# A two-layer decoder trunk on one core: sums of squares and the mean's spread moved to the matrix engine, convolution taps dealt out anew, the last output projection in halves, three row tiles at each feed-forward's end

## The chip, the cores and the metric

The kernel runs on one core of a Trainium2 chip. A core has a matrix engine (TensorE, PE in the rows), a vector engine (VectorE, DVE), a scalar engine (ScalarE, ACT) and a general engine (GpSimd, POOL), each with its own instruction stream; SyncE (SP) issues the transfers. Engines wait for each other by semaphores only. The metric is the time of one execution on the device, in microseconds (us); a kernel's time is the median of its runs.

## The reference

The input is 512 tokens of 1024 features in float32. Two mixers follow each other, a convolution module and an attention, each followed by a gated feed-forward; every one of the four blocks adds its result to its input, and normalises its input first.

```python
def rmsnorm(x, g):
    y = xf * lax.rsqrt(jnp.mean(xf * xf, axis=-1, keepdims=True) + EPS)
def conformer_conv(h, ...):
    u = h @ w_pw1 + b_pw1
    a, gate = jnp.split(u, 2, axis=-1)
    u = a * jax.nn.sigmoid(gate)
    u = causal_dwconv(u, w_dw, b_dw)          # 31 taps a channel
    u = jax.nn.silu(layernorm(u, ln_g, ln_b)) # mean and variance over features
    return u @ w_pw2 + b_pw2
```

The attention has 16 query heads in 4 groups of four, three branches merged by gates, and an output projection `w_out`. The feed-forward (2816 wide) has a gate, a causal convolution of width 3 and a down-projection back to 1024 features.

## The kernel before, in words

Features lie on the 128 partitions and the 512 tokens along the free axis, so an activation is eight tiles of 128x512, and `x[0..7]` is the residual stream. Every float32 product is made of three matmuls (`mm3`, L240 to L243): both operands are split into a rounded high part (a cast on ACT, L230, L236, L405, L616) and the remainder (a subtraction on DVE or POOL, L231, L237, L406, L617). PSUM tiles come from small rings named `pf`, `pb`, `pa` and `po`.

The Tile framework's scheduler sets the order on each engine: it plays the program through with costs of its own and puts on each engine what is ready first, so an edit at one place moves instructions at others.

- **Norms.** `Norm.add` scales and splits a row tile and squares it on ACT (L265). The first norm (`two=True`) sums the squares in two accumulators, three adds on POOL and three on DVE (L272). `sums` adds over features with one-column matmuls against `ones` (L285), four for each 128x512 tile. Then DVE and POOL make 1/sqrt (L293, L295), and `spread` (L306) transposes it into a row for all partitions.
- **Convolution module.** Eight units of 128 channels. `project_half` makes the first pointwise layer, `U.gate` and `U.unit` the gated input (L358, L364, L365). The 31 taps of a unit are dealt out by the table `CONV`: `pe` gives the groups of four taps that the matrix engine makes with diagonal weights (`products`), `pool` the taps of POOL (L388, from copies scaled by ACT at L386), and what is left goes to DVE (L354). `a`, `b`, `c` say how many DVE taps are written between other steps. `merge` (L436) joins the parts.
- **The convolution's layer norm.** One-column matmuls (L527) sum the last units' values and squares; three matmuls against `avg` (L529) make the mean, spread over the partitions, in `dp`. DVE, POOL and `spread(rs)` make 1/sqrt; `warm(w1)` and `warm(w2)` (L213, L211) put matmuls without use before and behind it. `centre` (L550) and `scale` (L554, L555) lead to the second pointwise layer.
- **Feed-forwards.** `down` makes a row tile of the down-projection in a `pb` bank; at each block's end two row tiles run together: first all products but the last column block, then, for both, the last one, which waits for the block's last activation (L236 from L631).
- **Attention.** A table deals out heads and projections over steps. `out_proj(n)` makes the output projection of one or two groups, row tile by row tile in a `pf` bank; `out2` is that of the last group, ready when both of its half-groups (`os`) are done. `out1` is that of group 2.

## Time and profile before

| | us |
|---|---|
| median of three runs | 1280.56 |
| lowest and highest run | 1279.15, 1282.36 |
| the profiled execution | 1281.02 |
| its span in the trace | 1279.1 |
| PE busy in the span | 1237.5 |
| DVE, ACT, POOL busy | 1008.7, 729.0, 370.4 |

Stages on PE: convolution module to about 190 us, first feed-forward to 553, attention to about 911 (its start overlaps the feed-forward's end), second feed-forward to the end. The profiled execution lies 0.46 us above the median, and 1.9 us of it are outside the span. Timeline rows give start, length, engine, line, operation, output<-inputs, shape, count, and in brackets the engine's idle time before it with what ended that. A float32 matmul with one column or a float32 transpose leaves two records each, so x8 at L285 or L527 is four instructions.

### The profile page before, as it was taken

Reading aid. Unit: us, or ns where it says so; the run is one execution under the profiler, and the core shown is the slowest. Engines: PE = TensorE matmul, PEld = TensorE weight load, DVE = VectorE, ACT = ScalarE, POOL = GpSimd, SP = SyncE. Lnnn points to the kernel's source line nnn. Section 1 sums busy time; section 2 is a strip of 40 time slices with the busy share of each in tenths; the row PEclk is TensorE's granted clock in tenths of the full one; section 3 lists DMA queues with packets and bytes.
Section 4 is the critical chain, followed back from the end, with each engine's and each line's share of the span. In section 5 each row is a group of like instructions: output and inputs, shape, how many; then the busy total and the mean of one; then the engine's idle time right before and its main releaser. Section 6 shows DMA issues by size and latency. Waiting matters only on the chain. (4 is left out here: it accounts for less than half of the span.)

```text
span 1279.1 us, 20179 instructions
## 1 busy us (share of the span) xinstructions
PE 1237.5 (97%) x7447; PEld 1089.2 (85%) x7447; DVE 1008.7 (79%) x1728; ACT 729.0 (57%) x1337; POOL 370.4 (29%) x434
## 2 busy tenths in 40 slices
PE   8999899999999999999889999999899999999998
PEld 6788778879999999978888987877687999999996
DVE  6699957689977787765868888889768997778873
ACT  5766545345654455453767888767544565455541
POOL 1639603001100010051657677634300110001100
PEclk8999989999999999999999999999899999999999
DMA  7555413223232333235431111111122333233321
GB/s 276 165 144 141 107 50 128 73 70 126 88 112 100 99 100 107 77 116 166 134 101 51 34 45 39 34 34 34 51 68 70 110 103 108 90 106 106 97 79 72
DMA packets 43794, 121.91 MB, mean 95 GB/s; under 512 B 5424, under 2 KB 8240, under 8 KB 43696
## 3 DMA queue, kind: packets, MB, share of 16 engines
q1 hardware_dynamic: 43696, 120.64, 30.0%
q8 instruction: 58, 0.95, 0.3%
q14 instruction: 40, 0.33, 0.1%
HBM read 108.04 MB, written 2.10 MB: 86 GB/s over the span
## 5 line engine op out<-in xcount | busy, mean ns | idle before, releaser
L700 POOL TENSOR_TENSOR S<-raw 128x512 f32<-128x512 f32 x34 | 52.8, 1553 | 516.3 <-DMA raw<-in_up_dram 266.0
L616 ACT CAST wh<-raw 128x1024 fp32r<-128x1024 f32 (+2 forms) x112 | 96.0, 863 | 90.3 <-PE pb L242 26.8
L617 DVE TENSOR_TENSOR wl<-raw,wh 128x1024 fp32r<-128x1024 f32 (+2 forms) x112 | 114.8, 1031 | 29.3 <-ACT wh L616 29.1
L241 PE MATMUL pf<-s,wh 128*128 128x512 f32 x296 | 116.8, 405 | 9.7 <-ACT s L236 4.6
L242 PE MATMUL pf<-s,wh 128*128 128x512 f32 x296 | 119.1, 403 | 0.0
L243 PE MATMUL pf<-s,wl 128*128 128x512 f32 x296 | 118.5, 400 | 0.0
L1149 POOL TENSOR_SCALAR s<-s,cf,gates 128x128 f32<-128x128 f32 (+3 forms) x128 | 81.0, 640 | 73.7 <-DVE cf L1146 59.1
L241 PE MATMUL pb<-s,wh 128*128 128x512 f32 x254 | 99.8, 396 | 2.5 <-ACT s L236 2.3
L242 PE MATMUL pb<-s,wh 128*128 128x512 f32 x254 | 100.2, 395 | 0.0
L243 PE MATMUL pb<-s,wl 128*128 128x512 f32 x254 | 99.8, 393 | 0.0
L230 ACT CAST wh<-raw 128x1024 fp32r<-128x1024 f32 (+2 forms) x62 | 63.5, 1024 | 41.5 <-PE pf L242 14.9
L241 PE MATMUL pf<-wh,s 128*128 128x256 f32 (+1 forms) x288 | 83.4, 290 | 3.6 <-DVE v L974 2.0
L1143 ACT ACTIVATE s<-pa,mn 128x128 f32<-128x128 f32 (+3 forms) x128 | 67.4, 531 | 30.4 <-DVE mn L1138 23.2
L242 PE MATMUL pf<-wl,s 128*128 128x256 f32 (+1 forms) x288 | 82.9, 288 | 1.8 <-POOL wl L231 1.4
L231 DVE TENSOR_TENSOR wl<-raw,wh 128x1024 fp32r<-128x1024 f32 (+2 forms) x46 | 60.9, 1325 | 28.6 <-ACT wh L230 28.6
L243 PE MATMUL pf<-wh,s 128*128 128x256 f32 (+1 forms) x288 | 82.4, 286 | 0.0
L241 PEld LDWEIGHTS pf<-s,wh 128*128 128x128 f32 x296 | 56.9, 193 | 23.8 <-ACT s L236 5.3
L236 ACT CAST s<-s 128x512 fp32r<-128x512 f32 x76 | 47.2, 621 | 50.8 <-DVE s L631 38.7
L750 DVE TENSOR_TENSOR x<-pb,x 128x512 f32<-128x512 f32 x80 | 54.0, 686 | 25.1 <-PE pb L243 25.0
L617 DVE TENSOR_TENSOR l<-raw,h 128x1024 fp32r<-128x1024 f32 (+2 forms) x56 | 57.3, 1024 | 17.5 <-ACT h L616 17.4
L1138 DVE CUSTOM_DVE_ANT_0 pa<-pa,tab 128x128 f32<-128x128 f32 (+3 forms) x128 | 62.5, 494 | 11.0 <-PE pa L1133 10.1
L237 DVE TENSOR_TENSOR s<-s,s 128x512 fp32r<-128x512 f32 x76 | 59.2, 779 | 13.9 <-ACT s L236 13.6
(299 smaller groups left out, 3957.7 us busy)
## 6 DMA issues: line engine op xcount, KB each, us to landing
raw<-in_up_dram SPq DMA_DIRECT2D x88, 512.0 KB, 3.6
raw<-in_dn_dram SPq DMA_DIRECT2D x48, 256.0 KB, 2.6
raw<-in_dn_dram SPq DMA_DIRECT2D x32, 320.0 KB, 2.8
raw<-in_pw_dram SPq DMA_DIRECT2D x16, 512.0 KB, 4.7
raw<-in_win_k_dram SPq DMA_DIRECT2D x8, 536.0 KB, 3.5
s<-s SPq DMA_DIRECT2D x32, 128.0 KB, 2.3
raw<-in_win_q_dram SPq DMA_DIRECT2D x8, 512.0 KB, 4.0
raw<-in_cw_dram SPq DMA_DIRECT2D x8, 512.0 KB, 3.4
```

What stands on the lines that cost most here:

```text
L230: nc.scalar.copy(h[:, :n], raw[:, :n])
L231: (eng or nc.vector).tensor_sub(l[:, :n], raw[:, :n], h[:, :n].bitcast(F32))
L237: nc.vector.tensor_sub(l, src, h.bitcast(F32))
L241: nc.tensor.matmul(out, ah, bh, start=start, stop=False)
L242: nc.tensor.matmul(out, ah, bl, start=False, stop=False)
L243: nc.tensor.matmul(out, al, bh, start=False, stop=stop)
L616: nc.scalar.copy(h, raw)
L617: (eng or nc.vector).tensor_sub(l, raw, h.bitcast(F32))
L750: nc.vector.tensor_add(x[m], o[m], x[m])
L1138: nc.vector.tensor_tensor_reduce(sv, sv, mask[:, S - n:S], 1.0, 3e38, op0=ALU.add, op1=ALU.min, accum_out=s.mn[:, c:c + 1])
L1143: nc.scalar.activation(a, sv, AF.Exp, scale=-1.0, bias=s.mn[:, c:c + 1], accum_out=s.sums[:, c:c + 1])
L1149: nc.gpsimd.tensor_scalar(a, a, s.cf[:, c:c + 1], gates[:, i, 3 * s.h + 1 + br:3 * s.h + 2 + br], op0=ALU.mult, op1=ALU.mult)
```

## The change

Five parts, with small changes of tables beside them. (1) In the first norm each squared tile is summed by four one-column matmuls at once; the six adds are gone. (2) `dp` is no longer a product with `avg`: the mean out of `mom` is transposed and spread like 1/sqrt, and the two fillers grow from 10 and 6 to 14 and 10. (3) `CONV` is dealt out anew: PE takes a seventh group of unit 6, POOL 38 taps where it had 47, DVE five more; the low parts of the diagonals of units 6 and 7 and of the first three weight blocks of the second pointwise layer (`"pw2": 3`) go from DVE to POOL. (4) `out_last` makes the last output projection four row tiles at a time, first with the first half-group for all four (three `pf` banks and one `pa`), then with the second, and may begin when the first half-group is done. (5) `TOGETHER = 3`: three row tiles at each feed-forward's end, the third in a `pf` bank.

```diff
-CONV = {"pe": [3, 2, 4, 4, 4, 4, 6, 5], "pool": [8, 8, 7, 6, 6, 6, 3, 3], ... "w1": 10, "w2": 6, ...}
+CONV = {"pe": [3, 2, 4, 4, 4, 4, 7, 5], "pool": [8, 8, 7, 4, 5, 2, 0, 4], ... "w1": 14, "w2": 10, ... "dp": [0, 0, 0, 0, 0, 0, 1, 1], "pw2": 3}
...
                 if s.two:
-                    if s.acc[k % 2] is None:
-                        s.acc[k % 2] = q
-                    else:
-                        (nc.vector if k % 2 else nc.gpsimd).tensor_add(s.acc[k % 2], s.acc[k % 2], q)
+                    s.sums(q, s.n == 1, s.n == KT)
...
-                s.sums(s.acc[0], True, False)
-                s.sums(s.acc[1], False, True)
+                if not s.two:
+                    s.sums(s.acc[0], True, False)
+                    s.sums(s.acc[1], False, True)
...
-                return load_split(A["pw2"][k], MF * P)
+                return load_split(A["pw2"][k], MF * P, nc.gpsimd if k < CONV["pw2"] else nc.vector)
...
-                nc.tensor.matmul(dp, avg, a, start=n == 0, stop=n == APART)
...
             dlt = mom[:, 0:NB]
+            dp = spread(dlt, "pa")
...
-                    o[m] = ps("pb")
+                    o[m] = ps("pb" if len(o) < 2 else "pf")
...
-            down(len(CHUNKS) - 1, 0, 1)
-            for m in range(2, KT):
+            down(len(CHUNKS) - 1, *range(TOGETHER))
+            for m in range(TOGETHER, KT):
                 down(len(CHUNKS) - 1, m)
...
+            def out_last(n):
+                os = Gs[OUTS[n][0]].os
+                for u in range(2):
+                    wh, wl = weights("wout", 2 * OUTS[n][0] + u)
+                    o = [None] * 4
+                    for p in range(2):
+                        while len(os) <= p:
+                            yield
+                        for m in range(4):
+                            if p == 0:
+                                o[m] = ps("pa" if m == 3 else "pf")
+                            b = (2 * m + p) * P
+                            mm3(o[m], wh[:, b:b + P], wl[:, b:b + P], os[p][0], os[p][1], p == 0, p == 1)
+                            if p:
+                                k = 4 * u + m
+                                nc.vector.tensor_add(x[k], o[m], x[k])
+                                nxt.add(k)
+                        yield
...
-                work[f"out{n}"] = out_proj(n)
+                work[f"out{n}"] = (out_last if n == len(OUTS) - 1 else out_proj)(n)
```

Where instructions move, the program's order shows it. **The start, on PE.** The names: `wh_126`, `wl_127` are the first weight block, `s_122`, `s_123` the parts of the first normalised tile, `po_135` the sums. Before:

```order
L241 MATMUL pf_121<-s_122,wh_126 128x512
L242 MATMUL pf_121<-s_123,wh_126 128x512
L243 MATMUL pf_121<-s_122,wl_127 128x512
L241 MATMUL pf_121<-s_135,wh_126 128x512
L242 MATMUL pf_121<-s_136,wh_126 128x512
L243 MATMUL pf_121<-s_135,wl_127 128x512
L241 MATMUL pf_121<-s_144,wh_126 128x512
L242 MATMUL pf_121<-s_145,wh_126 128x512
L243 MATMUL pf_121<-s_144,wl_127 128x512
L241 MATMUL pf_121<-s_154,wh_126 128x512
```

After, with L243 to L245 for what was L241 to L243 and L284 for L285:

```order
L243 MATMUL pf_121<-s_122,wh_126 128x512
L244 MATMUL pf_121<-s_123,wh_126 128x512
L284 MATMUL po_135<-ones,s_133 128x1 x4
L245 MATMUL pf_121<-s_122,wl_127 128x512
L243 MATMUL pf_121<-s_140,wh_126 128x512
L284 MATMUL po_135<-ones,s_147 128x1 x4
L244 MATMUL pf_121<-s_141,wh_126 128x512
L245 MATMUL pf_121<-s_140,wl_127 128x512
L243 MATMUL pf_121<-s_153,wh_126 128x512
L284 MATMUL po_135<-ones,s_160 128x1 x3
L244 MATMUL pf_121<-s_154,wh_126 128x512
L245 MATMUL pf_121<-s_153,wl_127 128x512
```

Before, the first sums stand some 60 rows further down and are eight in all; now there are 32, from the third matmul to the 50th row, and the transposes of 1/sqrt (L306) stand 26 rows behind the last of them.

**The end of the convolution, on PE.** `pb_1505` and `pb_1506` hold the sums, `pa_1506` before is `dp`. Before:

```order
L529 MATMUL pa_1506<-s_765,avg 128x512
L527 MATMUL pb_1505<-ones,s_765 128x1 x4
L527 MATMUL pb_1505<-ones,s_595 128x1 x4
L527 MATMUL pb_1505<-ones,y_1154 128x1 x4
L527 MATMUL pb_1505<-ones,s_1474 128x1 x4
L529 MATMUL pa_1506<-y_1154,avg 128x512
L527 MATMUL pb_1505<-ones,y_1306 128x1 x4
L527 MATMUL pb_1505<-ones,s_1479 128x1 x4
L529 MATMUL pa_1506<-y_1306,avg 128x512
L213 MATMUL pf_1544<-s_1479,ident 128x128 x10
L306 MATMUL po_1555<-ident,rs_1540 128x128 x4
```

After, where `pa_1533` is `dp`:

```order
L527 MATMUL pb_1506<-ones,s_783 128x1 x4
L527 MATMUL pb_1506<-ones,s_613 128x1 x4
L527 MATMUL pb_1506<-ones,y_1153 128x1 x4
L527 MATMUL pb_1506<-ones,s_1475 128x1 x4
L527 MATMUL pb_1506<-ones,y_1296 128x1 x4
L527 MATMUL pb_1506<-ones,s_1480 128x1 x4
L215 MATMUL pf_1546<-s_1480,ident 128x128 x10
L306 MATMUL pa_1533<-ident,mom_1531 128x128 x4
L215 MATMUL pf_1546<-s_1480,ident 128x128 x4
L306 MATMUL po_1561<-ident,rs_1542 128x128 x4
L213 MATMUL pf_1566<-idle 128x512 x10
```

The three products with `avg` are gone; four transposes of `mom` stand between two pieces of the first filler.

**The end of the attention, on PE.** `pf_9773` and `pf_9810` before are the last two row tiles of `out1`, `pb_9550` a transposed probability tile that waits for POOL's scaling (L1149). Before:

```order
L241 MATMUL pf_9773<-s_9394,wh_9668 128x512
L242 MATMUL pf_9773<-s_9395,wh_9668 128x512
L243 MATMUL pf_9773<-s_9394,wl_9669 128x512
L241 MATMUL pf_9810<-s_9060,wh_9668 128x512
L242 MATMUL pf_9810<-s_9061,wh_9668 128x512
L243 MATMUL pf_9810<-s_9060,wl_9669 128x512
L241 MATMUL pf_9810<-s_9394,wh_9668 128x512
L242 MATMUL pf_9810<-s_9395,wh_9668 128x512
L243 MATMUL pf_9810<-s_9394,wl_9669 128x512
L1157 MATMUL pb_9550<-ident,s_9343 128x128
L1157 MATMUL pb_9550<-ident,s_9341 128x128
L1157 MATMUL pb_9550<-ident,s_9344 128x128 x2
```

After, where `pb_9560` is that tile:

```order
L1173 MATMUL po_9440<-s_9471,v_5608 128x256
L1173 MATMUL po_9440<-s_9472,v_5608 128x256
L1133 MATMUL pa_9553<-wide_8745,s_9185 128x384
L1133 MATMUL pa_9553<-wide_8746,s_9185 128x384
L245 MATMUL pf_9753<-s_9404,wl_9679 128x512
L1157 MATMUL pb_9560<-ident,s_9353 128x128
L1157 MATMUL pb_9560<-ident,s_9351 128x128
L1157 MATMUL pb_9560<-ident,s_9354 128x128 x2
L1133 MATMUL pa_9569<-wide_8745,s_9185 128x384
L1133 MATMUL pa_9569<-wide_8746,s_9185 128x384
L1133 MATMUL pa_9598<-wide_8745,s_9185 128x512
L1133 MATMUL pa_9598<-wide_8746,s_9185 128x512
```

The twelve matmuls of the last two `out1` tiles are gone from here, since the new projection holds the `pf` banks; they stand 150 rows further down, behind the second half of `out_last`'s first tiles, and the last head's last scores (L1133 on `pa_9794`) stand 13 rows later than they did, behind the transposes and value products of the heads before.

## Rows read from the trace of the kernel before

**Rows 1.** The page's part 1: busy time of each engine, share, instructions.

```profile
PE 1237.5 (97%) x7447; PEld 1089.2 (85%) x7447; DVE 1008.7 (79%) x1728; ACT 729.0 (57%) x1337; POOL 370.4 (29%) x434
```

**Rows 2.** Windows: length, busy time (count) of PE, PEld, DVE, ACT, POOL, clock.

```profile
8.90:15.40 6.50, 6.46 (x14) 4.58 (x15) 6.16 (x7) 6.50 (x11) 2.27 (x2) 0.50 1.03 401
15.40:34.00 18.60, 16.48 (x80) 13.22 (x79) 13.77 (x16) 10.43 (x14) 3.05 (x3) 1.00 0.70 245
...
75.00:143.90 68.90, 68.82 (x298) 55.49 (x296) 67.91 (x85) 47.57 (x74) 57.28 (x62) 1.00 0.49 131
```

**Rows 3.** Timeline of PE, the first norm's sums and spread.

```profile
28.24 0.95 PE L285 MATMUL po<-ones,s 128*128 128x1 f32 x8
29.05 0.48 PE L243 MATMUL pf<-s,wl 128*128 128x512 f32 x1
...
31.52 0.65 PE L306 MATMUL po<-ident,nt 128*128 128x128 f32 x4 [0.59 <-POOL nt L295]
```

**Rows 4.** Timeline of PE, unit 7's products and what follows.

```profile
146.92 0.47 PE L241 MATMUL pa<-s,dh 128*128 128x512 f32 x1 [2.85 <-ACT dh L405]
148.15 0.47 PE L242 MATMUL pa<-s,dh 128*128 128x512 f32 x1 [0.75 <-POOL s L454]
...
150.02 0.62 PE L241 MATMUL pa<-s,dh 128*128 128x504 f32 x1
150.44 0.62 PE L242 MATMUL pa<-s,dh 128*128 128x504 f32 x1
...
156.39 1.02 PE L529 MATMUL pa<-s,avg 128*128 128x512 f32 x2
```

**Rows 5.** Groups of instructions by form, DVE, 75 to 165 us.

```profile
L406 DVE TENSOR_TENSOR dl<-dr,dh 128x1024 fp32r<-128x1024 f32 x4 | 6.4, 1595 | 0.0
L231 DVE TENSOR_TENSOR wl<-raw,wh 128x768 fp32r<-128x768 f32 x4 | 5.9, 1468 | 0.0
...
L354 DVE SCALAR_TENSOR_TENSOR pb<-s,vec,pb 128x484 f32<-128x484 f32 x7 | 5.0, 723 | 0.1
```

**Rows 6.** Timeline of DVE and PE, the layer norm at the convolution's end.

```profile
159.33 0.69 DVE L436 TENSOR_TENSOR y<-pb,y 128x512 f32<-128x512 f32 x1
...
162.76 1.85 PE L527 MATMUL pb<-ones,s 128*128 128x1 f32 x8
164.47 2.05 PE L529 MATMUL pa<-y,avg 128*128 128x512 f32 x2
166.32 3.71 PE L213 MATMUL pf<-s,ident 128*128 128x128 f32 x20
...
173.30 0.96 PE L241 MATMUL pf<-s,wh 128*128 128x512 f32 x3 [1.44 <-ACT s L236]
```

**Rows 7.** Timeline of PE, the first feed-forward's end and the attention's start.

```profile
550.54 0.73 PE L241 MATMUL pb<-s,wh 128*128 128x512 f32 x2 [1.17 <-ACT s L236]
...
552.78 0.50 PE L241 MATMUL pb<-s,h 128*128 128x512 f32 x1 [0.32 <-DVE x L750]
...
589.36 0.51 PE L241 MATMUL pf<-s,wh 128*128 128x512 f32 x1 [0.93 <-DVE s L846]
```

**Rows 8.** Timeline of PE, POOL and ACT, the attention's end.

```profile
882.47 0.60 PE L1157 MATMUL pb<-ident,s 128*128 128x128 f32 x4
...
881.32 1.09 POOL L1149 TENSOR_SCALAR s<-s,cf,gates 128x256 f32<-128x256 f32 x2 [3.22 <-DVE cf L1146]
...
892.52 0.50 PE L1166 MATMUL po<-s,s 128*128 128x512 f32 x1 [1.43 <-DVE s L1180]
...
897.97 0.62 PE L1133 MATMUL pa<-wide,s 128*128 128x512 f32 x2
...
900.12 0.30 PE L1157 MATMUL pb<-ident,s 128*128 128x128 f32 x1
...
908.79 1.99 ACT L616 CAST h<-raw 128x1024 fp32r<-128x1024 f32 x2
...
911.36 1.65 PE L241 MATMUL pf<-s,wh 128*128 128x512 f32 x3 [3.20 <-ACT s L236]
```

More of the change, by code (lines that the diff above doesn't have):

```diff
@@ L33 @@
 LATE = 0
+TOGETHER = 3
 NORM_AT = [(0, 5), (1, 3)]
@@ L46 @@
 NCTR = 2
-CONV = {"pe": [3, 2, 4, 4, 4, 4, 6, 5], "pool": [8, 8, 7, 6, 6, 6, 3, 3], "a": [10, 6, 5, 5, 3, 4, 5, 6, 8, 5], "b": [6, 4, 3, 4, 4, 5, 5, 5, 5, 4], "c": [3, 5, 2, 3, 3, 6, 5, 2, 4, 2], "w1": 10, "w2": 6, "d": [0, 0, 0, 0, 0, 0, 0, 0], "dp": [0, 0, 0, 0, 0, 0, 0, 0]}
+CONV = {"pe": [3, 2, 4, 4, 4, 4, 7, 5], "pool": [8, 8, 7, 4, 5, 2, 0, 4], "a": [10, 6, 6, 5, 4, 4, 5, 6, 8, 5], "b": [6, 4, 3, 4, 4, 5, 4, 5, 5, 4], "c": [1, 5, 1, 3, 3, 6, 4, 2, 4, 2], "w1": 14, "w2": 10, "d": [0, 0, 0, 0, 0, 0, 0, 0], "dp": [0, 0, 0, 0, 0, 0, 1, 1], "pw2": 3}
 HD = 64
@@ L90 @@
 WARM = 12
-FIRST_W = (0, 3)
+FIRST_W = [0, 3]
 LATE_SQ = 0
@@ L517, in second @@
             def second(k):
-                return load_split(A["pw2"][k], MF * P)
+                return load_split(A["pw2"][k], MF * P, nc.gpsimd if k < CONV["pw2"] else nc.vector)
             wp2 = [second(k) for k in range(4)]
             last = units[KT - 1]
-            st, dp = ps("pb"), ps("pa")
+            st = ps("pb")
             groups = [(stat["y"], stat["q"])] + [(units[c].y, units[c].q) for c in range(KT - APART, KT)]
@@ L1199, in out_proj @@
                     nc.vector.tensor_add(x[m], o, x[m])
-                    if n == len(OUTS) - 1:
-                        nxt.add(m)
                     yield
+            def out_last(n):
+                os = Gs[OUTS[n][0]].os
+                assert len(OUTS[n]) == 1 and len(os)
+                for u in range(2):
[14 more added lines that the diff above has]
+                        yield
             def drain(*gens):
@@ L1258, in ready @@
                 if nme[:-1] == "out":
-                    return len(Gs[OUTS[int(nme[-1])][-1]].os) == 2
+                    return len(Gs[OUTS[int(nme[-1])][-1]].os) >= (1 if int(nme[-1]) == len(OUTS) - 1 else 2)
                 if nme[:-1] == "kv" and int(nme[-1]) >= NVB:
```

## Prediction

> **What bounds the kernel now.** I read the busy times first. PE is busy 1237.5 us of its span [rows 1], so there is nothing to gain by relieving another engine except where PE waits for it; what PE does not do is 41.6 us, and each part of the change is worth the waits that it takes away, less the PE work that it adds. The windows by stage show where PE is full: from 75 to 143.9 us it works 68.82 of 68.90 us, 298 matmuls at 0.231 us, and DVE works 67.91 [rows 2]. The clock comes second: from 8.9 to 15.4 us the granted clock is 0.50 (1.2 GHz), then 1.00 (2.4 GHz). Last I read the timeline of PE around every edit, for the waits in brackets. The forecast is made against the profiled execution, 1281.02 us, which lies 0.46 us above the median, and is carried to the median at the end. A measurement of this kernel tells about 0.3% (3.8 us) from no change.
>
> **Part 1, the first norm's sums.** Added are 24 one-column instructions on PE. In the row of eight records (four instructions) the next matmul starts 0.81 us later, 0.20 us for one [rows 3]. About half of the 32 sums stand ahead of the clock's rise by their place in the order. At half clock four instructions take 164.47 - 162.76 = 1.71 us, 0.43 each [rows 6]; but in that time a wide matmul, 0.42 us at half clock (150.02 to 150.44) [rows 4], would have run, and is made up later at 0.231, so that one costs 0.23. Together 12 x 0.23 + 12 x 0.20 = 5.2 us. The ends: 24 x 0.20 = 4.9 us, and 24 x 0.43 = 10.3 us if none of it is made up. Taken away is PE's idle time there, 18.60 - 16.48 = 2.1 us [rows 2], the most visible piece being 0.59 us for POOL's 1/sqrt at 31.52 [rows 3]. In the new order 26 rows, 6.0 us, lie between the last sum and the transposes, and before the whole chain from the last sum to the transposes took 2.5 us (29.05 to 31.52), so the wait is covered. The squares come early enough, since ACT's order is as before. Net +3.1 us, all of it passed on, because PE is full from here to 143.9 us.
>
> What the row shows is 0.10 us for each record of one column. The Trainium skill (TensorE: Matmul & The Clock Gate, section Back-to-back issue gap) gives a floor of about 25 ns between matmuls of up to 64 columns, by which the 24, two records each, would cost 24 x 2 x 0.025 = 1.2 us, an estimate, and the part would gain 0.9 us. The trace disagrees: four times that, and its price is the one in the sum.
>
> **Part 3, the taps.** PE takes one group more, six matmuls, 6 x 0.231 = +1.4 us. PE then reaches unit 7's products at 143.9 + 3.1 + 1.4 = 148.4 us. Before, it stood there for 2.85 and 0.75 us, until 148.15, and the 29 matmuls that were left took until 156.39, 8.2 us where 29 x 0.231 = 6.7 would do, since the clock was down [rows 4]. DVE is relieved: four low parts of diagonals go, the two longest 1.6 us each, three low parts of weights at 1.47, for five taps more at 0.72: at least 3.2 + 4.4 - 3.6 = 4.0 us less [rows 5]. So what PE waited for is not later than at 148.15 and PE does not wait: -3.6 us of waits and -1.5 us of lost clock. POOL's new low parts lie where it loses nine taps; I cost them at nothing, and if they are late for a unit the old wait is back, at most 3.6 us. Products end at 156.39 + 3.1 + 1.4 - 3.6 - 1.5 = 155.8 us.
>
> **Part 2, the mean.** The last merge on DVE ended at 159.33 + 0.69 = 160.0 [rows 6], 3.6 us behind the products, a chain over ACT and DVE; with products at 155.8 it could end at 159.4, but DVE has one more addition there, and I leave it at 160.0. Behind it the sums ended at 164.47, with two products with `avg` and much at half clock [rows 6]. Now eight one-column instructions stand behind the merge: ACT's square and 1.6 us at full clock, 3.4 at half; I take 162.6, -1.9 us. Then before came `avg` (1.85 us) and the ten fillers (3.54, from 166.32 to 169.86), and then the spread of 1/sqrt. Now: ten fillers, 3.5 us, transposes of the mean, about 1.2, four fillers, 1.4, all at half clock: 6.1 for 5.4 us, +0.7; POOL's 1/sqrt is done within. If the clock rises in the midst, as it did before, 0.5 us less. The second pointwise layer starts at about 173.30 - 1.7 = 171.6 us. Ends of this part: -0.5 us, all at half clock with the merge late, to -4.5 us, all at full clock. The longer last filler only fills the wait of 1.44 us at 173.30. **Convolution: -1.7 us**, and this term, not +3.1, counts, because the layer norm's chain and not PE ends the module: behind the products PE has sixteen one-column sums ahead of the last merge's, 3.2 us, and so is at 159.0, 1.0 us before that merge; a PE that is later still shows beyond that.
>
> **Part 5, three row tiles.** At the first feed-forward's end PE waits 1.17 us for the last activation's split and 0.32 for an addition [rows 7]. Nine matmuls of the third tile, 2.1 us, stand between and cover both: -1.5 us. The second feed-forward's end shows the same two waits, and its order is otherwise unchanged: **-1.5 us** at the kernel's end. At the first, the attention follows, and the scheduler has placed the transposes of 1/sqrt two matmuls later and a cast of 1072 columns on ACT ahead of the copy that follows them. There PE waited 0.93 us for DVE (589.36) [rows 7]; the two matmuls no longer cover it (+0.46), and the cast, about 1 us, delays it further: +1.3 us. **-0.2 us** there; ends -1.5 and +0.5.
>
> **Part 4, the halves.** The twelve matmuls that are gone from before 882.47 are worth 12 x 0.231 = 2.8 us, but PE took up the next transposes at 882.47 and POOL's scaling for them ended at 881.32 + 1.09 = 882.41 [rows 8]: they covered a wait, which now opens, and nothing is won. DVE wins two additions there, which shorten later waits such as the 1.43 us at 892.52. The last head's scores, at 897.97, come three more matmuls of the half-projection later (0.7 us) and behind thirteen rows which before ran from 898.43 to 900.12 (1.7 us): +2.4, of which DVE's lead gives back about half: +1.2. From there a chain of waits runs to 911.36. On it ACT had two weight casts, 1.99 us, ahead of the last split (908.79); now one: -1.0. Behind it PE has twelve matmuls more and six fewer: +1.4. Sum **+1.6 us**. The ends: +2.8 (DVE's lead gives nothing), and -3.0 (the 2.8 us are won after all and, the wait of 3.20 us at 911.36 being shorter, the clock drops less).
>
> **Sum.** -1.7 - 0.2 + 1.6 - 1.5 = -1.8 us; 1279.2 for an execution like the profiled one, **1278.7 us** for the median. It is within 0.3%: the gains at the seams are real but each is 1 to 2 us, and two of them are given back where the order moved.
>
> **Rivals.** *Faster.* The gap before 882.47 does not open because POOL's scaling comes earlier with the lighter queues, and the layer norm's end keeps the full clock: -3.0 - 4.5 - 0.2 - 1.5 = -9 at the most, some -6 in the middle: 1274.5. For it speaks that the fillers are longer and that every wait named here is short; against it that POOL's result, not PE's work, ended the stretch before 882.47, and that the clock did fall while PE did one-column sums (the sums at 162.76 take twice those at 28.24). *Slower.* The one-column sums at the start hold the clock at half. Before, it rose at 15.4 us after wide matmuls alone; now every fourth instruction has one column, and the end of the module shows that a PE which is busy with such sums can stand at half. Each us of delay costs 0.46 us, since a wide matmul takes 0.42 for 0.231. If it lasts until the last sum, some 39 wide matmuls instead of 14 and all sums are at half: 25 x 0.19 + 20 x 0.23 = +9.4 us; PE then ends the convolution, and some +8 of it remain: 1287. It decides from a rise later than about 21 us (the 1.8 us of gain and 1.0 of slack, by 0.46). Against it: at 28 us eight records in a row left the clock of that window at 1.00 [rows 2]. *It does not do what it says.* The third tile and the halves leave their waits where they were, moved by a few matmuls: -1.7 + 1.3 + 1.6 = +1.2, 1281.8.
>
> **How the numbers follow.** The forecast case 0.43, from 1275.5 to 1281.5, 0.08 of it under the bound of 1276.7; the faster rival 0.32; the slower rival 0.14, 0.12 of it above 1284.4; no effect 0.11. Faster 0.08 + 0.32 = 0.40, slower 0.12, within 0.3% the remaining 0.48. The range, 1271.5 to 1285, leaves out the far half of each rival's reach, about 0.2.
>
> **What would show it.** Part 1: the idle time between 15 and 34 us gone, the first products with taps about 3 us later, the clock's rise at 15 to 16 us; later than 21 us and the slower rival holds. Part 3: no wait over 0.5 us before unit 7's products, and their end near 155.8. Part 2: the first product of the second pointwise layer near 171.6. Part 5: both waits before the last column block gone, a wait of about 2 us at the attention's fourth projection tile. Part 4: a wait of over 2 us for POOL before the transposes at 880 to 882, and the split that PE waits for at the end 0 to 1 us later than at 911.36. The forecast is wrong if that wait for POOL is absent, or if the layer norm at the convolution's end runs at full clock.

## The result, and the profile after

The changed kernel takes 1293.85 us in the median (1289.88 to 1298.67), the kernel before 1281.33 (1279.15 to 1282.36), both of six runs in one session: a ratio of 1.0105, with an interval from 1.0091 to 1.0118. It is slower by 1%; the prediction said 1278.7 and at most 1285. The profiled execution took 1294.8 us with a span of 1293.0, 13.9 us above the span before.

The page's busy line of the changed kernel, to be held against [rows 1]:

```profile
PE 1254.8 (97%) x7511; PEld 1108.5 (86%) x7511; DVE 1000.9 (77%) x1723; ACT 722.4 (56%) x1328; POOL 362.3 (28%) x428
```

DVE, ACT and POOL are relieved by 7.8, 6.6 and 8.1 us, as the change means them to be, and PE is busy 17.3 us longer, with 64 records more. Its idle time hardly changes (41.6 before, 38.2 now). So the loss is not in waits alone: PE spends longer on its work.

The windows of the changed kernel (length, busy time and count of PE, PEld, DVE, ACT, POOL, then the granted clock), which answer to [rows 2]:

```profile
8.90:15.40 6.50, 6.50 (x27) 5.89 (x25) 5.59 (x8) 6.50 (x12) 0.00 (x0) 0.50 1.04 410
15.40:34.00 18.60, 18.60 (x63) 16.28 (x64) 5.18 (x6) 5.01 (x9) 0.00 (x0) 0.50 0.48 180
75.00:143.90 68.90, 68.90 (x300) 56.12 (x299) 66.38 (x88) 42.74 (x64) 47.13 (x54) 1.00 0.55 150
```

The second row is the result in one line. PE is never idle from 15.4 to 34 us, as forecast, but the clock is 0.50 where it was 1.00. The timeline of PE in that stretch (L284 are the sums, L306 the transposes of 1/sqrt) goes with [rows 3]:

```profile
9.35 1.70 PE L284 MATMUL po<-ones,s 128*128 128x1 f32 x8
...
31.11 1.70 PE L284 MATMUL po<-ones,s 128*128 128x1 f32 x8
36.21 0.95 PE L284 MATMUL po<-ones,s 128*128 128x1 f32 x8
42.92 0.60 PE L306 MATMUL po<-ident,nt 128*128 128x128 f32 x4
```

Only the last four of the 32 sums run at full clock, behind 36 us; the transposes come at 42.92 instead of 31.52. The end of the convolution, PE, and after the dots DVE's last merge, goes with [rows 4] and [rows 6]:

```profile
157.99 0.47 PE L244 MATMUL pa<-s,dh 128*128 128x512 f32 x1 [0.75 <-DMA s<-s]
164.63 1.84 PE L527 MATMUL pb<-ones,s 128*128 128x1 f32 x16
169.05 1.87 PE L527 MATMUL pb<-ones,y 128*128 128x1 f32 x8 [0.80 <-DVE y L436]
172.49 3.97 PE L215 MATMUL pf<-s,ident 128*128 128x128 f32 x20
181.07 0.97 PE L243 MATMUL pf<-s,wh 128*128 128x512 f32 x3 [0.52 <-ACT s L238]
...
168.31 0.69 DVE L436 TENSOR_TENSOR y<-pb,y 128x512 f32<-128x512 f32 x1
```

Of the 11.4 us of delay at the transposes, 7.8 arrive at the second pointwise layer (181.07 for 173.30). The waits of 2.85 and 0.75 us ahead of unit 7's products have become one of 0.75. Further on, PE at the attention's fourth projection tile, at the first split and transposes of the second feed-forward's norm, and in that feed-forward ([rows 7], [rows 8]):

```profile
597.54 0.50 PE L243 MATMUL pf<-s,wh 128*128 128x512 f32 x1 [2.47 <-DVE s L846]
...
921.50 0.96 PE L243 MATMUL pf<-s,wh 128*128 128x512 f32 x3 [2.26 <-ACT s L238]
...
953.89 0.60 PE L306 MATMUL po<-ident,nt 128*128 128x128 f32 x4
...
1000.56 0.50 PE L243 MATMUL pb<-s,wh 128*128 128x512 f32 x1 [3.04 <-ACT s L238]
```

The wait of 3.04 us is new. The same product in the kernel before, the next wait on PE in either kernel, and the transposes before:

```profile
939.62 0.60 PE L306 MATMUL po<-ident,nt 128*128 128x128 f32 x4
...
986.00 0.40 PE L241 MATMUL pb<-s,wh 128*128 128x512 f32 x1
...
988.00 0.50 PE L685 MATMUL pa<-kept,wh 128*128 128x256 f32 x2 [0.44 <-ACT wh L616]
```

```profile
1003.33 0.80 PE L685 MATMUL pa<-kept,wh 128*128 128x256 f32 x2 [0.26 <-ACT wh L616]
```

Before, PE did not wait for that product at all. The windows of the changed kernel around its wait (length, PE's busy time and count, clock, then two columns on transfers) show what follows:

```profile
995.00:1000.00 5.00, 2.52 (x11) 1.00 0.18 74
1000.00:1005.00 5.00, 4.18 (x11) 0.67 0.00 0
```

So the loss has two places, as the same instructions before and after show (forecast and measured: how much later they start than before, in us):

| place on PE | before | forecast | measured |
|---|---|---|---|
| second pointwise layer | 173.30 | -1.7 | +7.8 |
| attention's fourth projection tile | 589.36 | -1.9 | +8.2 |
| last split of the attention | 911.36 | -0.3 | +10.1 |
| L685 in the second feed-forward | 988.00 | -0.3 | +15.3 |
| end of the span | 1279.1 | -1.8 | +13.9 |

From the start to the second pointwise layer 7.8 us are lost where 1.7 were to be won, and 5.2 us are lost inside the second feed-forward, which the prediction put at nothing. The stretches between (+0.4 and +2.0, forecast -0.2 and +1.6) and the end (-1.4, forecast -1.5) came out near their forecasts.

### The profile page after: what moved, and what is told of

Its sections match the earlier page's. It is cut to its first block, busy times and chain, and to the rows that moved or that the text cites. A ratio compares the mean times of both kernels' runs of the same rounds, so it can differ in the third digit from the quotient of the medians.

```text
span 1293.0 us, 20268 instructions
## 1 busy us (share of the span) xinstructions
PE 1254.8 (97%) x7511; PEld 1108.5 (86%) x7511; DVE 1000.9 (77%) x1723; ACT 722.4 (56%) x1328; POOL 362.3 (28%) x428
## 4 chain that ended last, share of the span: by engine, by line
PE 82%; DVE 7%; issue 4%; ACT 3%; POOL 2%; DMA 2%; SPq 0%; ACTq 0%; POOLq 0%; DVEq 0%
PE pa L685 14%; PE pf L243 7%; PE pf L685 7%; PE pf L244 7%; PE pf L245 7%; PE pb L243 6%; PE pb L244 6%; PE pb L245 6%; PE po L685 4%; PE pa L244 3%; PE pa L243 3%; PE pa L245 3%; PE po L1173 2%; PE pa L1133 2%; PE pb L1157 2%
## 5 line engine op out<-in xcount | busy, mean ns | idle before, releaser
L617 DVE TENSOR_TENSOR wl<-raw,wh 128x1024 fp32r<-128x1024 f32 (+2 forms) x112 | 116.7, 1046 | 30.5 <-ACT wh L616 30.3
L243 PE MATMUL pf<-s,wh 128*128 128x512 f32 x292 | 118.0, 413 | 7.7 <-ACT s L238 2.8
L245 PE MATMUL pf<-s,wl 128*128 128x512 f32 x292 | 119.0, 409 | 0.0
L243 PE MATMUL pb<-s,wh 128*128 128x512 f32 x254 | 100.0, 397 | 3.2 <-ACT s L238 3.0
L1149 POOL TENSOR_SCALAR s<-s,cf,gates 128x128 f32<-128x128 f32 (+3 forms) x128 | 81.5, 645 | 73.7 <-DVE cf L1146 58.9
L245 PE MATMUL pb<-s,wl 128*128 128x512 f32 x254 | 100.1, 394 | 0.0
L243 PE MATMUL pf<-wh,s 128*128 128x256 f32 (+1 forms) x288 | 83.4, 290 | 3.0 <-DVE v L974 2.4
L245 PE MATMUL pf<-wh,s 128*128 128x256 f32 (+1 forms) x288 | 82.2, 286 | 0.0
L243 PEld LDWEIGHTS pf<-s,wh 128*128 128x128 f32 x292 | 57.0, 196 | 21.7 <-ACT s L238 3.4
L617 DVE TENSOR_TENSOR l<-raw,h 128x1024 fp32r<-128x1024 f32 (+2 forms) x56 | 59.0, 1054 | 17.5 <-ACT h L616 16.4
```

Of the source, the lines that this page charges most:

```text
L243: nc.tensor.matmul(out, ah, bh, start=start, stop=False)
L245: nc.tensor.matmul(out, al, bh, start=False, stop=stop)
L617: (eng or nc.vector).tensor_sub(l, raw, h.bitcast(F32))
L1149: nc.gpsimd.tensor_scalar(a, a, s.cf[:, c:c + 1], gates[:, i, 3 * s.h + 1 + br:3 * s.h + 2 + br], op0=ALU.mult, op1=ALU.mult)
```

## The experiments

Differences are between medians, against runs of the kernel before in the same session (1280.2 to 1280.9 us). Where a run is compared with the changed kernel (1293.85), the two come from different sessions; the kernel before differs by up to 1.1 us between them.

### What the sums cost

The theory after the result was the prediction's own slower rival: one-column sums hold the clock at half. Its opponent: the wait of some 2 us behind the fillers at 8 us lets the clock fall, and the sums only happen to stand there.

**after_old_sums**: the changed kernel with the sums of the first norm as before.

```diff
-                    s.sums(q, s.n == 1, s.n == KT)
+                    if s.acc[k % 2] is None:
+                        s.acc[k % 2] = q
+                    else:
+                        (nc.vector if k % 2 else nc.gpsimd).tensor_add(s.acc[k % 2], s.acc[k % 2], q)
```

> The changed kernel with the first norm's sums undone (squares added by POOL and DVE again, eight one-column sums); all else as changed. Theory (the one-column sums between the first matmuls keep the granted clock at half until 35 us): the clock rises near 15.4 us as in the kernel before, unit 7's products end near 153 to 156 us instead of 164.6, and the time falls by 8 to 11 us against the changed kernel, to about 1284, which leaves about +3 over the kernel before. Rival (the sums cost only their own length, 5 us, less the 2 us of waits that they remove): 3 us less, about 1291.

Measured: 1281.02 us, ratio 1.000 (0.999 to 1.001). The clock is at 0.98 from 12 to 16 us, the transposes stand at 29.42, the second pointwise layer at 170.02. The sums thus cost 12.8 us in the changed kernel, as much as the whole result.

**before_new_sums**: the same edit the other way round, in the kernel before.

> The kernel before with the sums part alone. Theory: clock at half until some 35 us, PE reaches the first norm's spread 11 us later, and since the kernel before waits 3.6 us ahead of unit 7's products, part of that is taken up: 6 to 10 us slower, 1288 to 1291. Rival (own length only): 0 to +3 us.

Measured: 1285.87 us, ratio 1.005 (1.0024 to 1.0077), ten runs from 1281.5 to 1297.3. Its windows (length, PE, clock) and one block of sums:

```profile
16.00:20.00 4.00, 4.00 (x15) 0.56 0.97 386
20.00:24.00 4.00, 4.00 (x26) 1.00 0.78 247
```

```profile
28.61 0.95 PE L282 MATMUL po<-ones,s 128*128 128x1 f32 x8
```

In this profiled run the clock rises at about 19.5 us, half of the sums' records (32 of 64) run at 1.00 behind it, between wide matmuls as in the changed kernel, and the transposes come at 35.33. So the mixture does not hold the clock down whenever it stands there: it lets it rise early in one profile and late in another. The runs' mean clock over the whole span says the same: 0.990 in the fastest of the ten, 0.977 in the slowest. The same edit costs 5.0 us here and 12.8 in the changed kernel; the two profiled rises differ by some 16 us, which at the prediction's 0.46 us for each us of delay is an estimate of 7.4, near the difference of 7.8.

**after_long_warm**: the changed kernel with 18 fillers ahead of the first matmul (`WARM = 12` to `18`), so that PE doesn't stand for 2 us behind them.

> The changed kernel with 18 instead of 12 fillers at the very start, so that PE doesn't wait before the first product. In both kernels the granted clock is 1.00 during the fillers and falls to 0.50 after that wait of 2.2 to 2.6 us. Theory a (the wait lets the clock fall, and the sums only keep it from rising again): the clock is 1.00 from 8 us on, one-column sums between wide matmuls leave it there as the eight at 36 us did, and the time falls by 10 to 14 us, to about 1281. Theory b (one-column sums pull the clock down by themselves): it falls within the sums, and the time falls by 0 to 4 us.

Measured: 1291.15 us, ratio 1.0071 (1.0049 to 1.0092): only 2.7 us better than the changed kernel. The windows of this kernel (length, PE, clock):

```profile
8.00:12.00 4.00, 4.00 (x23) 1.00 1.04 386
12.00:16.00 4.00, 4.00 (x27) 0.77 1.00 382
16.00:20.00 4.00, 4.00 (x15) 0.50 1.04 399
...
28.00:32.00 4.00, 4.00 (x11) 0.59 0.40 131
```

PE is busy in every us of these rows, and the clock still falls from 1.00 to 0.50 once the sums begin (the first block stands at 10.90), and stays there to about 31. So the wait is not needed: the clock comes down while PE works on the sums without a gap.

**before_long_warm**: the same 18 fillers in the kernel before, as a control.

> The kernel before with 18 instead of 12 fillers at the very start. If the wait before the first product is what lets the clock fall: clock 1.00 from 8.9 us on where it is 0.50 until 15.4, 14 matmuls at 0.23 instead of 0.43 us, unless PE then waits for the squares and splits of the row tiles, which come at one in 1.1 to 2 us; 1 to 3 us at the start, of which the wait ahead of unit 7 eats most: 0 to 2 us faster. If it is not the wait: same time, clock 0.50 as before.

Measured: 1280.75 us, ratio 1.0005 (0.9996 to 1.0014). The clock is 1.00 from 0 to 44 us, and nothing is gained: PE then waits 0.71, 1.99 and 2.92 us at 13.14, 32.67 and 145.92, and reaches the second pointwise layer 1.0 us earlier only.

**after_late_sums**: the changed kernel with all 32 sums in one block behind 68 wide matmuls, held there by data that come from the last square.

```diff
-                    s.sums(q, s.n == 1, s.n == KT)
+                    s.acc.append(q)
...
+                if s.two:
+                    late = small(1, "late", 1)
+                    nc.vector.tensor_scalar(late, s.acc[-1][:, 0:1], 0.0, 1.0, op0=ALU.mult, op1=ALU.add)
+                    for k, q in enumerate(s.acc):
+                        s.sums(q, k == 0, k == KT - 1, late)
```

> The changed kernel with all 32 one-column sums in one block behind the first 68 wide matmuls (they multiply with a column of ones that depends on the last square), so that none stands between the first matmuls. Theory (place, not number: sums among the first matmuls keep the clock from rising): the clock is 1.00 from about 16 us to the block, the start costs the sums' length at full clock, 24 x 0.20 = 5 us, and up to 2 us of wait for 1/sqrt behind them; about 5 to 7 us over the changed kernel with its sums undone (1281.0), 1286 to 1288, and its runs lie within 3 us of each other. Rival (32 sums cost what they cost wherever they stand): 1291 to 1296.

Measured: 1294.07 us, ratio 1.0104 (1.0089 to 1.0119). I had expected the place to matter and not the number; that fell. PE's timeline, and the windows, of this kernel:

```profile
25.83 11.50 PE L284 MATMUL po<-late,s 128*128 128x1 f32 x64
```

```profile
24.00:28.00 4.00, 4.00 (x30) 1.00 0.27 77
28.00:32.00 4.00, 4.00 (x22) 0.52 0.60 234
32.00:44.00 12.00, 10.30 (x38) 0.50 0.13 44
```

From full clock, it falls to half within the block: 64 records take 11.5 us, where eight took 0.81 at full clock [rows 3], 6.5 for 64. The price is paid here too, though not all of it is the clock: from 32 to 44 us, behind the block, PE also stands still for 1.7 us.

**before_wide_dummies**: the kernel before with five products of 512 columns, of no use, among the first matmuls. This is extra PE work in the same place, but wide.

```diff
                 if s.two:
+                    if k in (0, 1, 2, 4, 6):
+                        nc.tensor.matmul(ps("pa"), avg, q, start=True, stop=True)
```

> The kernel before with five added 128x512 products of squares with the averaging matrix between the first matmuls, where the new sums stand; their result is used by nothing. At 0.86 us each at full clock they are 4.3 us, as long as 21 one-column sums. Theory (the column count is what keeps the clock down): the clock rises between 15 and 17 us in all runs, the spread of the first norm comes about 4 us later less the 0.6 us that PE waited there, and the time is 1283 to 1285 with its runs within 3 us of each other. Rival (any work that is added between the first matmuls delays the rise): times between 1281 and 1297 as with the new sums.

Measured: 1282.85 us, ratio 1.0011 (1.0002 to 1.0021), ten runs within 3 us of each other. The windows (length, PE, clock):

```profile
8.00:16.00 8.00, 7.48 (x29) 1.00 1.02 391
16.00:32.00 16.00, 15.51 (x74) 1.00 0.79 267
```

Extra wide work leaves the clock at 1.00 to 32 us and costs 2 us. What the sums cost beyond their own time is the clock, and wide matmuls in their place don't take it. Since the clock never fell in this profile before 32 us, the expected rise at 15 to 17 us was not put to the test.

### What the halves cost

The wait of 3.04 us in the second feed-forward stayed when the sums were undone (3.09 us at 988.09), so it had another cause.

**after_old_out**: the changed kernel with the output projection as before.

```diff
-                work[f"out{n}"] = (out_last if n == len(OUTS) - 1 else out_proj)(n)
+                work[f"out{n}"] = out_proj(n)
```

> The changed kernel with the last output projection row tile by row tile again. Theory (the halves delay the row tiles and with them the second feed-forward's norm, which opens a new wait of 3.04 us at 1000.6 us and a stretch of half clock behind it): that wait is gone, the time falls by 3 to 5 us, to about 1289 to 1291. Rival (the wait belongs to the third row tile or to the scheduler's order of the feed-forward): the wait stays, 0 to -1 us.

Measured: 1286.15 us, ratio 1.0033 (1.0013 to 1.0052), 7.7 us better than the changed kernel, and the wait is gone. The clock rises at 21 us in its profile and not at 35, so part of the 7.7 is the start's; its runs lie between 1281 and 1291. Against parts_that_gain (below), the same kernel without the new sums, it stands at +10.3 us, a third price of the sums beside 5.0 and 12.8.

**before_halves**: the halves alone, in the kernel before.

> The kernel before with the last output projection by halves alone. Theory (the halves make the row tiles late and the second feed-forward's norm with them): last split at the attention's end 0 to 1 us later, a wait of about 3 us about 79 us behind it, 3 to 5 us slower, about 1285. Rival (harmless by itself): within 1 us, no new wait in the second feed-forward.

Measured: 1286.62 us, ratio 1.0052 (1.0035 to 1.0068), +6.4 us. PE's timeline: the norm's transposes, and the wait; after the dots a window with its clock:

```profile
943.00 0.60 PE L306 MATMUL po<-ident,nt 128*128 128x128 f32 x4
...
989.67 0.50 PE L241 MATMUL pb<-s,wh 128*128 128x512 f32 x1 [3.09 <-ACT s L236]
...
990.00:995.00 5.00, 5.00 (x15) 0.66 0.00 0
```

The first split is at 910.62, no later than before; the transposes come 3.4 us later than the 939.62 of the kernel before; then comes the wait, and the clock falls behind it.

**before_halves_late**: the halves, but only after `out1` has ended, so that the twelve matmuls of [rows 8] stay where they were. A rival said that those made the difference.

```diff
             def ready(nme):
+                if nme == "out2" and "out1" in work:
+                    return False
```

> The kernel before with the halves, but these may begin only when the projection of group 2 is finished; its last twelve matmuls then keep their place, and the last scores stand where they stood. Theory (the halves are slow because they take the banks of those twelve matmuls, which then end the projection late, and the second feed-forward's norm with it): the wait of 3.09 us in the second feed-forward is under 1 us, the split that PE waits for at the attention's end comes 1 to 2 us earlier than with the halves of the change, and the time is 1279 to 1281. Rival (products by halves end all row tiles late by themselves, since four tiles run side by side): the wait stays and the time is 1285 to 1287.

Measured: 1285.27 us, ratio 1.0038 (1.0023 to 1.0053), and a wait of 3.05 us at 988.00. The moved matmuls are not the cause of the wait.

**halves_first_four** and **halves_last_four**: halves for four of the eight row tiles only, the others one by one. The diff is the first's; the second has `u == 1`. The theory was a burst: in halves four tiles end 0.7 us apart, and the next norm's squares come in a heap at the end.

```diff
                     o = [None] * 4
+                    for ms in (((0, 1, 2, 3),) if u == 0 else ((0,), (1,), (2,), (3,))):
...
-                        for m in range(4):
+                        for m in ms:
```

> The kernel before, with the last output projection by halves for its first four row tiles only; the last four are made one by one, as in the kernel before. Theory 'burst': what costs is that the last four row tiles end three matmuls (0.7 us) apart, while DVE needs about 1.8 us for a tile's addition and low part and ACT and POOL have their share; here they end six matmuls apart as before, so the norm's transposes come 28 to 29 us behind the first split as before, the wait near 988 us stays under 1 us, and the time is within 2 us of the kernel before. Rival 'anywhere': four banks held side by side, and the weight loads that come earlier, move the second feed-forward's splits; then 4 to 6 us slower, as with the full halves, and the 3 us wait is there.

> The kernel before, with the last output projection by halves for its last four row tiles only. Theory 'burst': the whole loss of before_halves is here, 4 to 6 us slower than before, with the norm's transposes some 30 to 32 us behind the first split and a wait of about 3 us near 988 us. Rival 'anywhere': the same as halves_first_four, within 1.5 us of it.

Measured: 1285.79 us, ratio 1.0044 (1.003 to 1.0059), and 1284.03 us, ratio 1.0026 (1.0014 to 1.0038). By the burst the first should have stayed within 2 us of the kernel before; it costs 5.1 us. The theory fell.

**halves_by_pairs**: two tiles at a time (`for ms in ((0, 1), (2, 3))`).

> The kernel before, with the last output projection by halves, two row tiles at a time: the tiles of a pair end 0.7 us apart, and the next pair 2.8 us later. Theory 'burst': DVE has only one tile more in hand than before, so 0 to 2 us slower. Rival 'anywhere': 3 us or more slower.

Measured: 1281.55 us, ratio 1.0008 (0.9999 to 1.0018). Its rows on PE, the transposes and the wait:

```profile
939.87 0.60 PE L306 MATMUL po<-ident,nt 128*128 128x128 f32 x4
...
988.71 0.51 PE L685 MATMUL pa<-kept,wh 128*128 128x256 f32 x2 [0.45 <-ACT wh L616]
```

Pairs lose next to nothing, and their transposes are not late. That left one question: does the late norm make the loss, or does it only go with four tiles side by side?

**norm_later_1** and **norm_later_3** leave the projection alone and make the last norm later, by two (five: `range(5)`) pairs of steps on POOL that add a number and take it away; the scheduler puts the transposes four (twelve) matmuls later. It also moves some matmuls of the second feed-forward on PE and steps on DVE, so the later norm is not all that differs.

```diff
+                if s.g == "g3":
+                    for _ in range(2):
+                        nc.gpsimd.tensor_tensor(m, m, mhalf[:, 0:NB], op=ALU.add)
+                        nc.gpsimd.tensor_tensor(m, m, mhalf[:, 0:NB], op=ALU.subtract)
                 nc.gpsimd.tensor_tensor(s.tok, m, mhalf[:, 0:NB], op=ALU.pow)
```

> The kernel before, with four small steps on POOL (add and subtract the same number, twice) ahead of the last norm's 1/sqrt. PE's rows are the same but for the norm's transposes, which stand four matmuls (0.9 us) later; the output projection is untouched. Theory 'later norm': the chain over DVE and ACT that starts at the transposes is as long as PE's work in the first half of the second feed-forward, so 0.9 us of delay opens a wait of about 0.9 us near 988 us and a part of the clock's fall: 1 to 3 us slower than before. Rival 'four tiles themselves' (banks and splits moved): within 0.5 us of before.

> The same with ten such steps: the transposes stand twelve matmuls (2.8 us) later, as in the full halves (3.4). Theory 'later norm': a wait of 2 to 3.5 us near 988 us, half clock behind it, 4 to 6 us slower than before, the whole price of the halves. Rival 'four tiles themselves': within 1 us of before.

Measured: 1280.92 us, ratio 1.000 (0.9991 to 1.0009), and 1284.78 us, ratio 1.0033 (1.0022 to 1.0044). The rows of norm_later_3 on PE, and a window:

```profile
942.42 0.60 PE L310 MATMUL po<-ident,nt 128*128 128x128 f32 x4
...
989.43 0.79 PE L241 MATMUL pb<-s,wh 128*128 128x512 f32 x1 [3.19 <-ACT s L236]
...
990.00:995.00 5.00, 5.00 (x13) 0.50 0.00 0
```

A later norm gives the same wait at the same place, the half clock behind it and 3.9 us of loss, with no tile of the projection moved. The smaller step was expected to cost 1 to 3 us and cost nothing. All the runs in one table, in order of PE's work from the transposes to the product that PE waits for (start of the product, less its wait, less the start of the transposes; without a wait the product starts at 986.71 in halves_by_pairs and 984.45 in norm_later_1):

| kernel | first split | transposes | PE's work to the product | PE's wait near 988 | clock, 990 to 995 | against before |
|---|---|---|---|---|---|---|
| halves_by_pairs | 912.54 | 939.87 | 46.8 | 0.45 (L685) | 1.00 | +0.8 |
| before | 911.36 | 939.62 | 46.4 | 0.44 (L685) | 1.00 | |
| norm_later_1 | 910.00 | 938.98 | 45.5 | 0.45 (L685) | 1.00 | +0.1 |
| halves_last_four | 913.19 | 942.24 | 44.7 | 1.58 | 0.69 | +3.3 |
| halves_first_four | 909.43 | 941.01 | 44.5 | 1.58 | 0.50 | +5.1 |
| before_halves_late | 912.20 | 940.69 | 44.3 | 3.05 | 0.90 | +4.4 |
| norm_later_3 | 911.51 | 942.42 | 43.8 | 3.19 | 0.50 | +3.9 |
| before_halves | 910.62 | 943.00 | 43.6 | 3.09 | 0.66 | +6.4 |

PE does not wait for the transposes themselves: it multiplies activations that are scaled only afterwards. But DVE's and ACT's whole chain of the feed-forward starts from them, and in the kernels that wait its first half ends 46.1 to 47.3 us later (the end of PE's wait less the transposes). In the kernel before PE takes up the same product at 986.00, 46.4 us behind the transposes, and the split that it needs ended at 985.57: two chains of one length side by side, with 0.4 us to spare. What counts is thus not the moment of the transposes but how much of PE's work the scheduler leaves behind them. So before_halves_late waits although its transposes stand 28.5 us behind the first split, about as before (28.3), and halves_last_four at 29.1, while norm_later_1, at 29.0, does not.

The chain itself is not of one length either. The split that PE needs ends 45.05 us behind the transposes in norm_later_1, 45.95 in the kernel before and 46.96 in norm_later_3. The wait of norm_later_3 adds up from the two: 2.6 us less work of PE behind the transposes and 1.0 us more chain, less the 0.4 to spare, make 3.2 of the measured 3.19 us. In norm_later_1 the shorter chain makes up for the later norm, which is why it cost nothing. DVE's rows show one difference: in the kernels with a wait of 3 us two low parts of weights (L617 in the kernel before, 1.23 us each) stand between the transposes and the first tile's gated product (L631), where the kernel before, halves_by_pairs and norm_later_1 have one. The later norm and the moved low part were not tried apart.

### What the other parts bring

**before_three_tiles**: `TOGETHER = 3` alone, with the third tile in a `pf` bank.

> The kernel before with three row tiles at both feed-forward ends alone. Theory (from the changed kernel's trace): the waits of 1.17 and 0.32 us are gone at both ends, the wait of 0.93 us at the attention's start becomes about 2.5: 1 to 2 us faster, 1279.5. Rival: the gain at the first end is given back more than once and the time is the same within 0.5 us.

Measured: 1278.78 us, ratio 0.9988 (0.9979 to 0.9998); the waits of [rows 7] at both ends are gone, that at the fourth projection tile is 2.47 us.

**before_conv_rest**: the new `CONV` table and the transposed mean, with the first norm as before.

> The kernel before with the convolution's other parts alone: the new table of taps, the mean by transposes, the longer fillers; sums, projection and feed-forwards as before. Forecast of the prediction without its first part: products of unit 7 end about 152.7 us, the module ends 1.7 us earlier, about 1279. Rival (the layer norm's chain of ACT, DVE and POOL, with POOL's new low parts on it, sets the end and has become longer: in the changed kernel the last merge came 4.4 us behind the products where it came 3.6 behind): the first product of the second pointwise layer is not earlier than 173.3, 0 to +2 us.

Measured: 1278.18 us, ratio 0.9983 (0.9973 to 0.9992); one wait of 0.75 us in unit 7, its products end at 153.49, the second pointwise layer starts at 170.85, 2.45 us earlier.

**parts_that_gain**: the changed kernel without the new sums and without the halves.

> The changed kernel with its sums and its halves undone: the convolution's other parts and the three row tiles. Both alone gave -2.2 and -1.5 us against the kernel before. If they add up: 3.7 us faster, about 1276.8. If one takes up the other's place: 1278 to 1279.

Measured: 1275.84 us, ratio 0.9958 (0.9941 to 0.9974), 5.0 us faster than the kernel before and 18.0 faster than the changed one. It beats both.

**gain_first_four**: the same with halves for the first four row tiles.

> The changed kernel with the first norm's sums as before and with halves for the first four row tiles only: parts_that_gain plus halves_first_four. Theory 'burst': about the time of parts_that_gain, 5 us faster than the kernel before, give or take 1.5 us. Rival 'anywhere': no gain left, within 1 us of the kernel before, as after_old_sums.

Measured: 1281.64 us, ratio 1.0009 (0.9999 to 1.0019). Even half of the halves takes the whole gain. PE waits 1.58 us for the product here too, but in this profile the clock behind the wait stays at 1.00 (990 to 995), where it fell to 0.50 in halves_first_four: the half clock does not follow every such wait.

## Why the prediction was wrong

**Part 1 is the step that failed first.** It let the clock rise at 15.4 us as before, with "about half of the 32 sums" ahead of that rise "by their place in the order". The rise came near 35 us, when 28 of them were done, at 0.43 us each (1.70 for four), and the wide matmuls between them ran at half clock too. The sums' own price was about right: with the rise at 19.5 us the transposes came 3.8 us late (before_new_sums, 35.33 for 31.52) for the term's 3.1. The slower rival had the mechanism and the size (it left some +8 of its +9.4 at the end of the convolution; 7.8 are measured at the second pointwise layer) and its own deciding point, a rise later than 21 us, was passed by 14 us. It got 0.14 because of one row: eight records at 28 us with the clock of that window at 1.00 [rows 2, 3]. That window holds 80 records, sixteen of them of one column and all of these behind 10 us of wide work at full clock; it says nothing of sums that stand ahead of the rise. The row that was like the new order was the sums at 162.76 at half clock [rows 6]. The prediction names it as a sign in both rivals, but its sum uses it as a price alone. The term was +3.1 and is 12.8 in the changed kernel (after_old_sums).

The Trainium skill (TensorE: Matmul & The Clock Gate, section What's actually happening) says that activity releases the throttle. Here PE was 100% busy by the profile while its clock went from 1.00 to 0.50 (after_long_warm, after_late_sums), so by the profile's busy time the rule is not borne out. The same section puts the cost of the ramp below 1% of a typical span and advises against fitting it. In size the trace agrees: of the 11.4 us at the transposes 4.9 are the 24 added sums at full clock, so at least 6.5 are the clock's, 0.5% of the span; but that is more than all the change was forecast to win, and it varies between runs.

**Part 4 was costed at the wrong place.** At the attention's end the forecast of +1.6 was near (+2.0 from 589.36 to 911.36), though not by its working: the wait of over 2 us for POOL before the transposes at 880 to 882 did not come (the waits there are 0.76 and 0.43 us for ACT). What was missed is the second feed-forward, which the prediction passed over without a term. There the halves cost 5.2 us in the changed kernel and 6.4 alone, through a later norm, a wait of 3 us and, in most of the profiles, a half clock behind it; no term of the sum stood for it. The chain from the norm's transposes to the first half's last activation was in the trace of before, with PE's 46.4 us beside it; its 0.4 us of slack could have been read.

**Parts 2 and 3 were near, with more in hand than forecast.** One wait of 0.75 us is left before unit 7, where none over 0.5 was to stand, and alone the two parts bring 2.0 us (before_conv_rest) for the forecast 1.7. On an undelayed start the second pointwise layer begins at 170.0 (after_old_sums) where the forecast, with its +3.1 at the start, had 171.6. In the changed kernel unit 7's products end 8.2 us late (164.63 for 156.39), the last merge follows 4.4 us behind them (3.6 before), and the delay goes through to the second pointwise layer; the 1.0 us that the prediction put between PE and that merge does not hide it.

**Part 5 was right.** -1.4 us alone, -1.4 at the end of the changed kernel for the forecast 1.5, and the wait at the fourth projection tile 2.47 us for "about 2".

Of the forecast's error of 15.7 us in the span, 9.5 stand ahead of the second pointwise layer and 5.2 in the second feed-forward. Not settled is how the parts add up: tiles and convolution together bring 5.0 us where alone they bring 3.4, and with the halves added the kernel stands at +0.1 where the sum of the three would be +3.0.

## What to carry to other kernels

A one-column matmul isn't priced by its own duration alone: many of them together took the clock from the wide matmuls around them here, in some runs for longer than in others, so look for a stretch of the trace with the same mixture and read its clock, not its length. When an edit moves the end of a block, follow the next norm on to where its chain next meets PE; where two chains of one length run side by side, 3 us of delay became 3 us of wait, often with a half clock behind it. Try the parts of a change apart: here two of five lost 5 to 13 us each and hid a version that is 0.4% faster than the kernel before.

## What the runs showed of the hardware

The granted clock fell from 1.00 to 0.50, the lower of its two levels (1.2 and 2.4 GHz), while PE was never idle, during one-column float32 matmuls alone (64 records, 11.5 us) or mixed with wide ones (after_long_warm, 12 to 16 us); with wide work in their place it stayed at 1.00 to 32 us (before_wide_dummies). It did not fall in every such mixture: in before_new_sums 32 one-column records ran among wide ones at 1.00 behind 20 us. What decides between the two is not shown, nor whether it is the single column or the load of a new operand ahead of each that counts.

With such sums at the start the time changes from run to run, and the mean clock with it: before_new_sums spreads over 15.8 us, its clock from 0.990 to 0.977; before_wide_dummies spreads over 3, from 0.993 to 0.989. The moment of the rise is seen only in the profiled runs: 19.5 us (before_new_sums), 21 (after_old_out), 31 (after_long_warm), 35 (the changed kernel).

A start at full clock is worth nothing by itself: before_long_warm holds 1.00 from the first microsecond on and takes the same time, since waits for other engines take its gain.
